# Moving where the pairs' hi and lo halves start in their tiles: 400 bytes below the whole tile's place instead of 64

## The chip, the cores and the metric

The kernel runs on one core of one Trainium2 chip. The metric is the device time of one launch in microseconds, over several runs. A profiled execution has its own time beside them, and a trace of every instruction of the engines: TensorE (PE, with its weight loads listed apart as PEld), VectorE (DVE), ScalarE (ACT), GpSimd (POOL) and SyncE (SP, which issues the DMAs).

## What is computed

One layer of an encoder on 256 tokens of width 4096, all in float32. The stream is layer-normed, multiplied by a wide input matrix, used in two branches (a gated convolution over three tokens, and windowed attention with 16 query heads), multiplied by an output matrix, added to the stream and normed again. Cut to what matters here:

```
h = layer_norm(x, emb_ln_g, emb_ln_b)              # 256 x 4096
p = h @ w_in                                       # 4096 x 13312 weights (26 column chunks of 512)
y_conv = c_b * conv3(c_c * c_h, conv_w) * silu(c_z)
y_attn = window_attention(q, k, v, sink) * silu(a_z)
y = concatenate([y_conv, y_attn]) @ w_out          # 4096 x 4096 weights
out = layer_norm(2**0.25 * h + y, ln_g, ln_b)
```

## The kernel before

Nearly all the work is the two products with `w_in` and `w_out`. The matrices arrive from memory in pieces of 128 x 2048 float32 (1 MB), each a tile `w0`, `w1`, ... of 8192 bytes in each of the 128 partitions. To keep float32 precision with the faster `float32r` matmul, every number is split in two: `hi`, the value rounded to float32r, and `lo`, what is left. ACT writes `hi` (`split_hi`, line 205) and DVE writes `lo = w - hi` (`split_lo`, line 209). The stream is split in the same way once and lies in `xT`. A product then takes three matmuls: x_hi by w_hi, x_hi by w_lo, x_lo by w_hi. In each, a 128 x 128 block of the stream is the stationary operand (the weights that PE loads), and 512 or 256 columns of `hi` or `lo` are the moving operand that streams past it.

Two kinds of steps follow each other in an order written out by hand (`ORDERS`, `OUT_ORDERS`):

- A whole step (`mm`, lines 251 to 253, and `mm_out`, lines 917 to 919) takes a whole piece of 2048 columns. In 512-wide column chunks that is 24 matmuls with 512 moving columns; in the last two output chunks, 256 columns wide, it is 48 matmuls with 256.
- A pair step (`mm_pair`, lines 275 to 277) multiplies two rows of blocks by a scheme with seven block products in place of eight. Its piece is loaded as four blocks of 256 columns, DVE adds four more blocks of sums beside them (`sums`, lines 182 to 184), and of the eight blocks the last seven (1792 columns) are split and used. The step is 21 matmuls with 256 moving columns. Their stationary operands are blocks of `xT` or of sums of it (`SC`, `SCy`).

Each chunk of the convolution branch is a row of whole steps (s), pair steps (S) and one half step (h): `sSShSsSSsSSs`. There are 185 pair steps in the kernel.

The `whi` and `wlo` tiles are three buffers each, used in turn, all of 8192 bytes. The split of step j + 3 stands behind the matmuls of step j on its engines, so ACT can write a `whi` buffer only when PE has finished with the step that used it, and DVE follows ACT.

The change touches where in these tiles a pair writes. Its seven blocks are read from column 256 (1024 bytes) of the `w` tile, and written `SHIFT` columns lower:

```
def dst(j, t):
    return t[:, HW - SHIFT:8 * HW - SHIFT] if is_pair(j) and len(raw[j].shape) == 2 else part(j, t)
...
c0 = HW if len(raw[j].shape) == 3 else HW - SHIFT
wh[j], wl[j] = wh[j][:, c0:c0 + 7 * HW], wl[j][:, c0:c0 + 7 * HW]
```

`HW` is 256, so with `SHIFT = 16` the seven blocks start at column 240 (960 bytes). A whole step's halves start at column 0. In the built program every `w`, `whi` and `wlo` buffer starts 384 bytes above a multiple of 512, and so does every stationary operand of these matmuls (the blocks of `xT`, `SC` and `SCy`).

Of the kernel before, what the change touches and what calls it, by code (L numbers as in the profile page):

```python
# [47 lines left out]
OP = 4  # L48
OUT_ORDERS = ["s" * 8] * 2 + ["sSsSsSsSss"] * 5 + ["", ""]
N_W = 3  # L50
SHIFT = 16


def units(ci):
# [45 lines left out]
def encoder_kernel(ctx: ExitStack, tc: tile.TileContext, x, emb_g, emb_b, wi, ws, conv_w, sink, wo, ln_g, ln_b, out):  # L100
# [85 lines left out]
    def part(j, t):  # L186

        if len(raw[j].shape) == 3:
            return t if len(t.shape) == 3 else t.rearrange("p (i n) -> p i n", i=2)
        return t[:, HW:] if is_pair(j) else t[:, 0:4 * HW] if steps[j][0] == "half" else t  # L190

    def dst(j, t):

        return t[:, HW - SHIFT:8 * HW - SHIFT] if is_pair(j) and len(raw[j].shape) == 2 else part(j, t)

# [11 lines left out]
    def split_lo(j):  # L207
        wl[j] = half_tile(j, "wlo")
        nc.vector.tensor_tensor(dst(j, wl[j]), part(j, raw[j]), dst(j, wh[j]).bitcast(F32), op=ALU.subtract)  # L209
        if is_pair(j):  # L210
            c0 = HW if len(raw[j].shape) == 3 else HW - SHIFT
            wh[j], wl[j] = wh[j][:, c0:c0 + 7 * HW], wl[j][:, c0:c0 + 7 * HW]
# [917 lines left out]
```

## Time and profile before

| | us |
|---|---|
| median of 3 runs | 1528.76 (1528.3 to 1529.1) |
| time of the profiled execution | 1529.49 |
| its span, first to last instruction | 1527.8 |
| PE busy, matmuls | 1511.7 (99%) |
| DVE busy | 1329.4 (87%) |
| ACT busy | 780.7 (51%) |

The clock granted to PE was 1.000 over the span. A matmul's busy time is longer than its place in the stream, because matmuls overlap and their ends are modelled: the distance from one matmul's start to the next one's start is what a matmul costs, and the timeline shows it.

### The profile page before, as it was taken

The page shows a single profiled execution, that of the slowest core. Times are in us where ns is not written, and L with a number is a line of the kernel's source. Part 1 is how long each engine was busy: PE and PEld are TensorE (multiplying, and loading weights), DVE is VectorE, ACT ScalarE, POOL GpSimd, SP SyncE. Part 2 cuts the span into 40 slices and gives each one's busy share as a digit, 9 for nine tenths or more (in the row PEclk, how much of TensorE's full clock was granted, in tenths as well). Part 3 has the DMA queues.
Part 4 walks back from the last instruction along what each step waited for, and adds up shares of the span by engine and source line. Part 5 has one row for each costly group of instructions (what it writes and reads, how often), then busy time and mean ns, then how long its engine had stood idle before and what let it go on. Part 6 is the DMA issues. An engine that isn't in the chain of part 4 may idle for free.

```text
span 1527.8 us, 21818 instructions
## 1 busy us (share of the span) xinstructions
PE 1511.7 (99%) x8879; PEld 1330.0 (87%) x8879; DVE 1329.4 (87%) x1555; ACT 780.7 (51%) x669; POOL 1.3 (0%) x7
## 2 busy tenths in 40 slices
PE   7999999999999999999999999999999999999998
PEld 4888989898988989989889888888988888888897
DVE  7769899999899898998898899989898688888876
ACT  5545546657565655545555455544556444444431
POOL 0000000000000000000000000000000000000000
PEclk9999999999999999999999999999999999999999
DMA  7555654555654556656555655556557655666573
GB/s 289 208 179 193 207 207 162 205 179 196 210 182 171 185 185 205 230 183 234 199 190 202 215 189 202 207 175 234 198 203 291 257 200 215 257 213 214 215 248 131
DMA packets 71716, 315.65 MB, mean 207 GB/s; under 512 B 8544, under 2 KB 12608, under 8 KB 50880
## 3 DMA queue, kind: packets, MB, share of 16 engines
q1 hardware_dynamic: 70608, 312.43, 58.4%
q10 hardware_dynamic: 1008, 1.84, 0.3%
q8 instruction: 69, 1.13, 0.3%
q14 instruction: 31, 0.25, 0.0%
HBM read 305.23 MB, written 8.91 MB: 206 GB/s over the span
## 4 chain that ended last, share of the span: by engine, by line
PE 83%; DVE 12%; ACT 2%; DMA 1%; issue 1%; SPq 0%; ACTq 0%; DVEq 0%
PE acc L252 13%; PE acc L253 13%; PE acc L251 13%; DVE wlo L209 7%; PE acc L918 6%; PE acc L919 6%; PE acc L917 6%; PE pacc L275 4%; PE pacc L277 4%; PE pacc L276 4%; PE acc L275 3%; PE acc L277 3%; PE acc L276 3%; ACT whi L205 2%; DVE w L182 1%
## 5 line engine op out<-in xcount | busy, mean ns | idle before, releaser
L205 ACT ACTIVATE whi<-w 128x2048 fp32r<-128x2048 f32 (+1 forms) x354 | 621.5, 1756 | 621.8 <-DVE w L184 218.2
L209 DVE TENSOR_TENSOR wlo<-w,whi 128x2048 fp32r<-128x2048 f32 (+1 forms) x354 | 736.4, 2083 | 123.7 <-ACT whi L205 123.5
L251 PE MATMUL acc<-whi,xT 128*128 128x512 f32 x988 | 387.4, 392 | 0.0
L252 PE MATMUL acc<-wlo,xT 128*128 128x512 f32 x988 | 386.0, 391 | 0.3
L253 PE MATMUL acc<-whi,xT 128*128 128x512 f32 x988 | 385.1, 390 | 0.0
L252 PEld LDWEIGHTS acc<-wlo,xT 128*128 128x128 f32 x988 | 185.5, 188 | 39.4 <-DVE wlo L209 3.6
L253 PEld LDWEIGHTS acc<-whi,xT 128*128 128x128 f32 x988 | 185.4, 188 | 38.1
L251 PEld LDWEIGHTS acc<-whi,xT 128*128 128x128 f32 x988 | 185.5, 188 | 35.0
L918 PE MATMUL acc<-wlo,xT 128*128 128x512 f32 (+1 forms) x480 | 175.1, 365 | 1.0 <-DVE wlo L209 1.0
L917 PE MATMUL acc<-whi,xT 128*128 128x512 f32 (+1 forms) x480 | 175.1, 365 | 0.0
L919 PE MATMUL acc<-whi,xT 128*128 128x512 f32 (+1 forms) x480 | 174.9, 364 | 0.0
L182 DVE TENSOR_TENSOR w<-w 128x512 f32<-128x512 f32 x179 | 122.3, 683 | 10.2 <-DMA w<-in_ws 10.2
L918 PEld LDWEIGHTS acc<-wlo,xT 128*128 128x128 f32 x480 | 90.6, 189 | 15.3 <-DVE wlo L209 1.7
L275 PE MATMUL acc<-whi,xT 128*128 128x256 f32 x370 | 103.7, 280 | 0.0
L276 PE MATMUL acc<-wlo,xT 128*128 128x256 f32 x370 | 103.7, 280 | 0.0
L277 PE MATMUL acc<-whi,xT 128*128 128x256 f32 x370 | 103.7, 280 | 0.0
L919 PEld LDWEIGHTS acc<-whi,xT 128*128 128x128 f32 x480 | 90.5, 189 | 14.3
L917 PEld LDWEIGHTS acc<-whi,xT 128*128 128x128 f32 x480 | 90.6, 189 | 13.9 <-issue 0.4
L275 PE MATMUL pacc<-whi,xT 128*128 128x256 f32 x350 | 99.8, 285 | 0.0
L276 PE MATMUL pacc<-wlo,xT 128*128 128x256 f32 x350 | 98.3, 281 | 0.0
L277 PE MATMUL pacc<-whi,xT 128*128 128x256 f32 x350 | 98.1, 280 | 0.0
L277 PE MATMUL pacc<-whi,SC 128*128 128x256 f32 x330 | 92.5, 280 | 0.0
(230 smaller groups left out, 2059.4 us busy)
## 6 DMA issues: line engine op xcount, KB each, us to landing
w<-in_wi SPq DMA_DIRECT2D x112, 1024.0 KB
w<-in_ws SPq DMA_DIRECT2D x202, 512.0 KB
w<-in_wo SPq DMA_DIRECT2D x41, 1024.0 KB
R<-in_wo SPq DMA_DIRECT2D x13, 1024.0 KB
x<-in_x SPq DMA_DIRECT2D x7, 512.0 KB
yl<-yd SPq DMA_DIRECT2D x7, 512.0 KB
xc<-in_x SPq DMA_DIRECT2D x14, 256.0 KB
R<-in_ws SPq DMA_DIRECT2D x6, 512.0 KB
```

The source lines that it names most:

```text
L182: nc.vector.tensor_tensor(s01, b22, b12.to_broadcast([P, 2, HW]), op=ALU.add)
L205: nc.scalar.activation(dst(j, wh[j]), part(j, raw[j]), AF.Copy)
L209: nc.vector.tensor_tensor(dst(j, wl[j]), part(j, raw[j]), dst(j, wh[j]).bitcast(F32), op=ALU.subtract)
L251: nc.tensor.matmul(a, xh, hk, start=(first and k == 0), stop=False)
L252: nc.tensor.matmul(a, xh, lk, start=False, stop=False)
L253: nc.tensor.matmul(a, xl, hk, start=False, stop=(last and k == PK - 1))
L275: nc.tensor.matmul(o, ah, hi[:, w - 1, :], start=(opens and p == 0), stop=False)
L276: nc.tensor.matmul(o, ah, lo[:, w - 1, :], start=False, stop=False)
L277: nc.tensor.matmul(o, al, hi[:, w - 1, :], start=False, stop=(closes and last))
L917: nc.tensor.matmul(o, yh, hk, start=first, stop=False)
L918: nc.tensor.matmul(o, yh, lk, start=False, stop=False)
L919: nc.tensor.matmul(o, yl, hk, start=False, stop=last)
```

## The change

One constant. A pair's `hi` and `lo` start at column 156 of their tiles (624 bytes) instead of column 240 (960 bytes). The same instructions stand in the same order on every engine, with the same waits; only the addresses differ that ACT and DVE write, that DVE reads of `whi`, and that PE reads as moving operand in the pairs' matmuls. Before, the moving operand of a pair's matmul starts 320 bytes above a multiple of 512 (64 bytes below the stationary operand's 384); now it starts 496 bytes above one (112 bytes above the stationary operand's). Before, it starts at a multiple of 64 bytes; now 48 bytes above one. Whole steps are as they were.

```
 OUT_ORDERS = ["s" * 8] * 2 + ["sSsSsSsSss"] * 5 + ["", ""]
 N_W = 3
-SHIFT = 16
+SHIFT = 100
```

## Prediction

> **What bounds the kernel.** I read the page first: busy times, then the chain of work that ended last, then the list of waits.
>
> ```profile
> PE 1511.7 (99%) x8879; PEld 1330.0 (87%) x8879; DVE 1329.4 (87%) x1555; ACT 780.7 (51%) x669; POOL 1.3 (0%) x7
> PE 83%; DVE 12%; ACT 2%; DMA 1%; issue 1%; SPq 0%; ACTq 0%; DVEq 0%
> ```
>
> ```profile
> ACT whi L205 <- PE acc L253: 172.7, 80, 3.7
> ...
> DVE wlo L209 <- ACT whi L205: 127.3, 101, 3.5
> ...
> PEld acc L252 <- DVE wlo L209: 3.6, 12, 0.4
> ```
>
> PE is busy 1511.7 of 1527.8 us. The waits turn in a ring: ACT waits for PE to give a `whi` buffer back (172.7 us here alone), DVE waits for ACT (127.3 us), and PE hardly waits for DVE (3.6 us in 12 waits). So the speed of the ring is PE's, and what a matmul costs in the stream is what counts. That is not its busy time but the distance between starts, so I went to the timeline of PE. First a pair step as most of them look, from its first matmul to the instruction behind it:
>
> ```profile
> 218.10 0.28 PE L275 MATMUL pacc<-whi,xT 128*128 128x256 f32 x1
> ...
> 218.45 0.28 PE L275 MATMUL acc<-whi,xT 128*128 128x256 f32 x1
> ...
> 220.45 0.28 PE L277 MATMUL pacc<-whi,SC 128*128 128x256 f32 x1
> 220.57 0.38 PE L490 MATMUL att<-ident,q 128*128 128x128 f32 x2
> ```
>
> Its 21 matmuls take 2.47 us. Between the fourth and the last start lie 17 steps in 2.00 us, 117.6 ns each. Now a pair step behind the attention's matmuls:
>
> ```profile
> 326.05 0.28 PE L275 MATMUL pacc<-whi,xT 128*128 128x256 f32 x1
> ...
> 326.40 0.28 PE L275 MATMUL acc<-whi,xT 128*128 128x256 f32 x1
> ...
> 328.33 0.28 PE L277 MATMUL pacc<-whi,SC 128*128 128x256 f32 x1
> 328.44 0.49 PE L490 MATMUL att<-ident,q 128*128 128x128 f32 x3
> ```
>
> The same code and the same addresses take 2.39 us, and the 17 steps take 1.93 us, 113.5 ns each. So a pair has two steady paces. Sorting all 185 pair steps by the median of their start distances gives 155 at the slow pace (117 to 118 ns) and 30 at the fast one (113 to 114 ns). The slow ones are those that PE enters straight out of a running stream of whole steps; the fast ones stand behind a break (a wait, transposes, the attention's matmuls). And here are matmuls of the same width, 256 columns, in a whole step of the last chunks, whose moving operand is not shifted:
>
> ```profile
> 1476.81 0.28 PE L917 MATMUL acc<-whi,xT 128*128 128x256 f32 x1
> ...
> 1478.49 0.28 PE L919 MATMUL acc<-whi,xT 128*128 128x256 f32 x1
> ```
>
> 14 steps in 1.68 us are 120.0 ns each, and they stay there. A whole step of 512 columns has one pace as well:
>
> ```profile
> 215.60 0.39 PE L252 MATMUL acc<-wlo,xT 128*128 128x512 f32 x1
> ...
> 217.87 0.39 PE L253 MATMUL acc<-whi,xT 128*128 128x512 f32 x1
> ```
>
> 10 steps in 2.27 us, 227 ns. From 120.0 to 227, 256 more columns cost 107 ns, so a 256-column matmul streams for some 107 ns and the rest is lost between or inside: 13 ns with the moving and the stationary operand at the same place modulo 512 bytes, 11 ns at the slow pace of the pairs, 6.5 ns at the fast one. My reading is that the next matmul's weight load, which runs under the current matmul's stream, gets in that stream's way where both reach for the same part of the memory, and that where they meet depends on the distance of their addresses and on the phase in which PE arrives.
>
> **The change part by part.** *PE, the moving operand's start.* 155 x 21 = 3255 matmuls at the slow pace and 630 at the fast one read from another place. No row shows a moving operand at this distance from the stationary one (112 bytes above, 48 past a multiple of 64), so the price is bounded. From below: no loss at all would be 107 ns. From the rows, the fastest steady pace is 113.5 ns. From above: 120.0 ns, the row at distance 0. I take the fast pace, 113.5 ns, because the current distance already admits it and only the phase in which the whole steps hand over keeps 155 pairs from it, and a distance that is no multiple of 64 puts the meeting points elsewhere; it is a choice between near rows, not a proof.
>
> The sum, by chunks of the convolution branch (7 pairs in 4 uninterrupted rows of one or two): the first pair of a row gains 2.47 - 2.39 = 0.08 us, since entering costs some slower matmuls; the three others gain 21 x (117.6 - 113.5) = 0.09 us. That is 0.59 us a chunk. The way back costs something. Here a whole step follows a fast pair:
>
> ```profile
> 223.30 0.28 PE L277 MATMUL pacc<-whi,SC 128*128 128x256 f32 x1
> 223.41 0.39 PE L251 MATMUL acc<-whi,xT 128*128 128x512 f32 x1
> ...
> 225.24 0.39 PE L253 MATMUL acc<-whi,xT 128*128 128x512 f32 x1
> ```
>
> Its first 8 steps take 1.83 us, where 8 x 0.227 = 1.82, so 0.01 to 0.03 us for each of 4 returns; 0.47 to 0.55 us a chunk are left. Behind 585 us, before the output, there are 89 slow pairs, 12.7 chunks' worth: 6.0 to 7.0 us. Before 585 us there are 46, or 6.6 chunks' worth: 3.1 to 3.6 us, of which I keep half, by the next paragraph: 1.6 to 1.8 us. In the output product 20 pairs stand one by one: 20 x (0.08 - 0.02) = 1.2 us. Together 8.8 to 10.0 us; I take 9.
>
> *What takes the place of PE's time.* A faster PE meets DVE next. The stretches of the attention, the convolution and the output:
>
> ```profile
> 252.00:378.00 126.00, 125.33 (x797) 113.10 (x796) 116.11 (x144) 80.00 (x86) 0.00 (x0) 1.00 0.58 196
> 924.00:1092.00 168.00, 167.93 (x1025) 150.09 (x1024) 151.97 (x166) 85.11 (x57) 0.00 (x0) 1.00 0.59 202
> 1260.00:1352.00 92.00, 92.00 (x495) 79.83 (x494) 80.94 (x87) 41.34 (x27) 0.00 (x0) 1.00 0.60 217
> ```
>
> The columns are the stretch, then busy us of PE, weight loads, DVE, ACT and POOL. In the convolution DVE has 16.0 us of 168 free, and PE would give back some 2 of them: it fits. In the attention DVE has 9.9 of 126 free, but its work comes in bursts and PE already loses 0.67 us there, so half is what I keep.
>
> *ACT and DVE, the new address.* 185 splits on each engine write from byte 624 instead of 960.
>
> ```profile
> L209 DVE TENSOR_TENSOR wlo<-w,whi 128x1792 fp32r<-128x1792 f32 x179 | 360.9, 2020 | 40.5 <-ACT whi L205 40.5
> L209 DVE TENSOR_TENSOR wlo<-w,whi 128x2048 fp32r<-128x2048 f32 x152 | 347.6, 2287 | 80.5 <-ACT whi L205 80.3
> ...
> L209 DVE TENSOR_TENSOR wlo<-w,whi 128x1024 fp32r<-128x1024 f32 x23 | 28.1, 1220 | 2.7 <-ACT whi L205 2.7
> ...
> L713 DVE SCALAR_TENSOR_TENSOR t<-att,cw,t 128x255 f32<-128x255 f32 x16 | 7.7, 483 | 0.6
> L711 DVE SCALAR_TENSOR_TENSOR t<-att,cw,t 128x255 f32<-128x255 f32 x16 | 7.6, 475 | 0.0
> ```
>
> A column costs (2287 - 1220) / 1024 = 1.042 ns; the shifted form should then take 1220 + 768 x 1.042 = 2020 ns, which it does. So the present shift between the `w` tile and the halves costs DVE nothing. Line 711 writes its tile from 4 bytes in, line 713 from its start, and the first is not slower (475 against 483 ns): an odd start costs DVE nothing either. I put both engines at 0, covered besides by the free time above; 1% on each split would be 20 ns of DVE in a pair and stay under that cover.
>
> **A rule weighed.** The rows above give one instruction stream 113.5, 117.6 or 120.0 ns at the same width. The Trainium skill ("SBUF — State Buffer", section "Who interferes with whom") gives PE two independent read ports, one for the moving operand and one for the weight load, and says that PE never waits on anyone; by that rule the address would not matter and the time would stay where it is. The trace speaks against it in so far as the pace differs between places, but no run yet moves the place alone. The Trainium skill ("TensorE: Matmul & The Clock Gate", section "Back-to-back issue gap") also gives 262 cycles for 256 columns, an estimate of 109 ns; by it the pairs could gain at most twice what I sum.
>
> **The rivals.**
>
> *The address is indifferent (1528.8 us).* Then 120.0 and 117.6 differ for another reason: the pairs write two halves of an accumulator in turn and change their moving block every matmul, the whole steps don't. For it: the slow pace of the pairs comes out the same for all their blocks and all their stationary operands. Against it: the two paces at one address show that something in the stream's phase costs 4 ns. It also holds if the interference repeats every 64 bytes or less and the rest of the shift is of no account. This is the rule of the two ports above.
>
> *The new place is as bad as none (slower, 1539 us).* If what matters repeats every 128 bytes, the old distance of 64 was the farthest from a meeting and the new one, 112, lies only 16 from one: the pairs then run at 120.0 ns like the unshifted row, with one pace only. Price: 3255 x (120.0 - 117.6) = 7.8 us and 630 x (120.0 - 113.5) = 4.1 us, together 11.9; of the second part some is hidden where PE waits for DVE anyway, so 10 us. It decides from 118.4 ns upwards (3885 x 0.8 ns = 3.1 us). A start that is no multiple of 64 bytes may also cost an additional access in each matmul. If one costs as much as the step from the fast to the unshifted pace, 6.5 ns, on top of the slow pace, that is 3885 x 6.5 = 25 us, 1554 us. I leave that end outside of the range.
>
> *More is gained.* With 107 ns the pairs would gain 3885 x 10 = 39 us by PE alone; DVE's free time would be used up long before (16.0 of 168 us), and a halved loss, 110 ns, would give some 17 us, 1512 us.
>
> **How the numbers follow.** Pairs at the fast pace or better: 0.44. Indifferent: 0.25. As bad as unshifted: 0.24; worse still: 0.07. A measurement of this kernel tells 0.2%, 3.1 us, from no change, so these are 0.44 faster, 0.25 same, 0.31 slower. The sum is made on the profiled execution (1529.49 us, 0.7 above the median of 1528.76): 9 us less than the median is 1519.8. For that case alone the range is 1512 to 1525; with the slower case it reaches from 1512 to 1540.
>
> **What would show it.** In the new trace the distance between starts in pair steps: 113.5 ns in those that follow whole steps means the forecast, 117.6 the first rival, 120.0 the second. The whole steps must stay at 227 ns and the splits at 2020 ns. If the pairs are at the fast pace and the time has not moved, waits of PE for `wlo` will have grown in its place. I am wrong if the interference has another period than I take it to have, which no row here can tell.

## The result, and the profile after

The changed kernel takes 1526.12 us (median of 22 runs, 1525.42 to 1526.76) where the kernel before takes 1528.78 (22 runs, 1528.01 to 1529.36). The ratio is 0.9983, with a 95% interval of 0.9976 to 0.9989: 2.66 us faster. That is 0.17%, a gain that can be told from none, but less than a third of the 9 us forecast. The profiled execution has a span of 1524.0 us, 3.8 below the one of before, at the same granted clock of 1.00.

The page, busy times and shares of the chain that ended last:

```profile
PE 1506.1 (99%) x8879; PEld 1320.3 (87%) x8879; DVE 1329.3 (87%) x1555; ACT 781.2 (51%) x669; POOL 1.3 (0%) x7
PE 81%; DVE 13%; ACT 2%; issue 1%; DMA 1%; SPq 0%; ACTq 0%; DVEq 0%
```

DVE's busy time has not changed, and its share of the chain went from 12 to 13%. First the pace, in the timeline of PE: the same pair step as the first one in the prediction, from its first matmul over the twelfth to the last.

```profile
217.76 0.28 PE L275 MATMUL pacc<-whi,xT 128*128 128x256 f32 x1
...
219.05 0.28 PE L277 MATMUL acc<-whi,xT 128*128 128x256 f32 x1
...
220.07 0.28 PE L277 MATMUL pacc<-whi,SC 128*128 128x256 f32 x1
...
223.06 0.39 PE L251 MATMUL acc<-whi,xT 128*128 128x512 f32 x1
...
224.90 0.39 PE L253 MATMUL acc<-whi,xT 128*128 128x512 f32 x1
```

It is entered straight out of whole steps. The first 11 distances average 1.29 / 11 = 117 ns, the last 9 are 1.02 / 9 = 113.3. So PE now finds the fast pace from there too, but not at once: about the first ten distances swing between 114 and 121 ns before they settle. Of 185 pairs 163 have a median of 113 to 114 ns (30 before), the other 22 lie at 115 to 118. The last two rows are the whole step behind the second pair of the row: 8 steps in 1.84 us, where 8 x 0.2267 is 1.81, so a return costs 0.03 us.

All of these 22 stand behind a break, and 18 of them were fast before. This is the pair behind the attention's matmuls that the prediction shows at 326.05, now with its first and twelfth matmul, its last, and the instruction behind it:

```profile
325.72 0.28 PE L275 MATMUL pacc<-whi,xT 128*128 128x256 f32 x1
...
327.02 0.28 PE L277 MATMUL acc<-whi,xT 128*128 128x256 f32 x1
...
328.04 0.28 PE L277 MATMUL pacc<-whi,SC 128*128 128x256 f32 x1
328.16 0.60 PE L490 MATMUL att<-ident,q 128*128 128x128 f32 x4
```

It took 2.39 us and takes 2.44: its first 11 distances average 1.30 / 11 = 118 ns, and only then does it reach 113.3. So the pairs that were fast already have become slower, by 0.04 us each in the mean of the 30.

The splits on DVE, groups with the shapes kept apart (busy us and mean ns behind the bar):

```profile
L209 DVE TENSOR_TENSOR wlo<-w,whi 128x1792 fp32r<-128x1792 f32 x179 | 360.9, 2020 | 38.7 <-ACT whi L205 38.7
L209 DVE TENSOR_TENSOR wlo<-w,whi 128x2048 fp32r<-128x2048 f32 x152 | 347.7, 2287 | 80.0 <-ACT whi L205 79.7
```

2020 and 2287 ns, as before. The new address costs DVE nothing. Now the waits (who waits, for whom; us in all, times, the longest in us), and behind them two rows of the kernel before that the prediction had no use for:

```profile
ACT whi L205 <- PE acc L253: 171.2, 80, 3.7
DVE wlo L209 <- ACT whi L205: 123.3, 94, 3.5
PEld acc L252 <- DVE wlo L209: 7.7, 27, 0.7
PE att L601 <- DVE s L567: 1.7, 4, 0.4
PEld att L616 <- DVE pT L608: 1.6, 5, 0.7
PE acc L252 <- DVE wlo L209: 1.5, 4, 0.4
```

```profile
PE att L601 <- DVE s L567: 1.3, 4, 0.3
PEld att L616 <- DVE pT L608: 1.2, 4, 0.6
```

PE's weight loads wait for `wlo` 27 times for 7.7 us, where it was 12 times and 3.6 us; its matmuls wait 4 times more, for 1.5 us. The attention's matmuls (lines 601 and 616) wait longer for DVE as well.

I summed the distances between the starts of all of PE's matmuls in both traces, by stretch: the pair steps without their waits, what a whole step has above 226.7 ns without a wait, the waits inside the products, and the other matmuls (attention, transposes) with their waits. The changes, in us:

| | attention | convolution | output | all |
|---|---|---|---|---|
| pair steps | -2.02 | -5.85 | -1.10 | -8.97 |
| waits inside the products | +0.49 | +3.12 | -0.68 | +2.94 |
| whole steps above their pace | +0.28 | +0.78 | +0.40 | +1.41 |
| other matmuls | +0.85 | +0.03 | -0.02 | +0.95 |
| together | -0.40 | -1.91 | -1.39 | -3.66 |
| forecast, returns taken off | -1.6 to -1.8 | -6.0 to -7.0 | -1.2 | -8.8 to -10.0 |

(The last column takes in 0.05 us of the prologue.) The row of the pair steps can't be held against the last row as it stands, since the forecast already has the returns taken off and half of the attention left out. Before that, the prediction's sum for the pair steps was 3.9 us in the attention (6.6 x 0.59), 7.5 in the convolution (12.7 x 0.59) and 1.6 in the output (20 x 0.08), 13.0 together; 8.97 came. Of these, 5.3 us were lost again, most of it as waits for DVE in the convolution.

One place shows how such a wait grows. Two timelines around one whole step of the convolution, the third step of a row of half step, pair and whole step. Before, DVE, ACT and PE:

```profile
960.50 0.42 DVE L184 TENSOR_TENSOR w<-w 128x256 f32<-128x256 f32 x1
...
962.84 2.02 DVE L209 TENSOR_TENSOR wlo<-w,whi 128x1792 fp32r<-128x1792 f32 x1 [0.77 <-ACT whi L205]
...
968.50 1.28 DVE L684 TENSOR_TENSOR tm<-acc,tm 128x512 f32<-128x512 f32 x2
```

```profile
961.10 1.71 ACT L205 ACTIVATE whi<-w 128x1792 fp32r<-128x1792 f32 x1 [1.75 <-DVE w L184]
```

```profile
968.18 0.39 PE L251 MATMUL acc<-whi,xT 128*128 128x512 f32 x1
968.64 0.50 PE L252 MATMUL acc<-wlo,xT 128*128 128x512 f32 x1
```

After, DVE and PE:

```profile
961.09 2.03 DVE L209 TENSOR_TENSOR wlo<-w,whi 128x1792 fp32r<-128x1792 f32 x1 [0.78 <-ACT whi L205]
...
964.55 2.29 DVE L209 TENSOR_TENSOR wlo<-w,whi 128x2048 fp32r<-128x2048 f32 x1
966.75 1.28 DVE L684 TENSOR_TENSOR tm<-acc,tm 128x512 f32<-128x512 f32 x2
```

```profile
966.12 0.40 PE L251 MATMUL acc<-whi,xT 128*128 128x512 f32 x1
966.89 0.50 PE L252 MATMUL acc<-wlo,xT 128*128 128x512 f32 x1 [0.37 <-DVE wlo L209]
```

From the point at which ACT lets it go, DVE works without a gap for 968.50 - 962.84 = 5.66 us before and 966.75 - 961.09 = 5.66 after: one pair's `lo`, the next pair's three sums, the whole step's `lo`. PE starts that whole step 5.34 us behind the same point before, and 5.03 after. It wants `wlo` one matmul later and gets it 5.80 us behind that point in both. The 0.31 us that PE gained on the way became 0.31 us of waiting. And the idle time ahead of DVE's stretch (0.77 and 0.78 us) is no reserve: the pair's sums end on DVE at 960.92, ACT makes `whi` of them from 961.10 to 962.81, and only then can DVE go on. It is ACT's passage in a chain from DVE to ACT and back to DVE.

### The profile page after: what moved, and what is told of

It is laid out like the page before. It is cut to its first block, busy times and chain, and to the rows that moved or that the text cites. A ratio compares the mean times of both kernels' runs of the same rounds, so it can differ in the third digit from the quotient of the medians.

```text
span 1524.0 us, 21818 instructions
## 1 busy us (share of the span) xinstructions
PE 1506.1 (99%) x8879; PEld 1320.3 (87%) x8879; DVE 1329.3 (87%) x1555; ACT 781.2 (51%) x669; POOL 1.3 (0%) x7
## 3 DMA queue, kind: packets, MB, share of 16 engines
q10 hardware_dynamic: 1008, 1.84, 0.3%
## 4 chain that ended last, share of the span: by engine, by line
PE 81%; DVE 13%; ACT 2%; issue 1%; DMA 1%; SPq 0%; ACTq 0%; DVEq 0%
PE acc L252 13%; PE acc L253 12%; PE acc L251 12%; DVE wlo L209 8%; PE acc L918 6%; PE acc L919 6%; PE acc L917 6%; PE pacc L277 4%; PE pacc L276 4%; PE pacc L275 4%; PE acc L276 3%; PE acc L275 3%; PE acc L277 3%; ACT whi L205 2%; DVE w L182 1%
## 5 line engine op out<-in xcount | busy, mean ns | idle before, releaser
L209 DVE TENSOR_TENSOR wlo<-w,whi 128x2048 fp32r<-128x2048 f32 (+1 forms) x354 | 736.4, 2083 | 120.6 <-ACT whi L205 119.6
```

## The experiments

Theory 1 was, at first, that the pairs gained what was forecast and that DVE's bursts took it back. Theory 2, that the loss lies elsewhere, so that the change would give as little on a kernel with less work for DVE.

**DVE relieved at the chunks' borders.** The adds that recombine the pairs, the convolution's side taps and the gate product are left out, and ACT copies the pairs' accumulators instead; once with the old place and once with the new.

```
     def pair_copy(ci):
-        nc.scalar.activation(e[:, 0, 0:HW], pacc[ci, 0][:, 0, :], AF.Copy)
+        for k in range(2):
+            nc.scalar.activation(e[:, k, :], pacc[ci, k].rearrange("p a b -> p (a b)"), AF.Copy)
     def pair_sums(ci):
-        ...
+        for k in range(2):
+            pacc.pop((ci, k))
```

> SHIFT 16 with DVE relieved: the recombination of the pairs' products (four adds of 256 columns a chunk), the two side taps of the convolution and the last gate product are left out; ACT copies the pairs' sums instead. Work on PE and the addresses stay. It is the base for the same kernel with SHIFT 100. Both theories: pairs as in the kernel before (155 at 117.8 ns, some 20 to 30 at 113.3), time 1520 to 1528 us, since PE waits little for DVE before the change.

> The same leaving out, SHIFT 100. Theory 1 (PE gave back 9 us in the pairs; where the convolution's chunks have their bursts of DVE work PE now waits 3.1 us longer for wlo, and 1.5 us go into the whole steps that follow a fast pair): with DVE relieved the waits do not grow, and it is 6 to 7.5 us faster than the relieved kernel with SHIFT 16. Theory 2 (the gain is lost in PE's own stream, by entering and leaving the fast pace, or in DMA): DVE's work is of no account, and the difference is 2.5 to 4 us as with the work in.

Measured: 1525.22 us (ratio 0.9977, interval 0.9967 to 0.9987) with the old place and 1521.77 (0.9954, 0.9942 to 0.9967) with the new, so the shift gives 3.45 us here, not the 6 to 7.5 of theory 1; that is a time of theory 2. DVE's busy time fell by 61 us, but PE's waits tell that it was not the time that counted. The row of each, old place first:

```profile
PEld acc L252 <- DVE wlo L209: 2.0, 7, 0.3
```

```profile
PEld acc L252 <- DVE wlo L209: 5.8, 30, 0.5
```

The waits inside the convolution's products grew with the shift again, from 2.50 to 4.52 us. What was left out stood at the chunks' borders, and the bursts in their middle stayed. With the waits still growing, this pair of runs does not decide between the theories, and the next pair was made to take DVE's work away where the waits are.

**DVE relieved inside the chunks.** As above, and `lo` is written for four of a pair's seven blocks only; the other three matmuls use those again.

```
+        if is_pair(j) and len(raw[j].shape) == 2:
+            nc.vector.tensor_tensor(dst(j, wl[j])[:, 0:4 * HW], part(j, raw[j])[:, 0:4 * HW],
+                                    dst(j, wh[j])[:, 0:4 * HW].bitcast(F32), op=ALU.subtract)
...
-            nc.tensor.matmul(o, ah, lo[:, w - 1, :], start=False, stop=False)
+            nc.tensor.matmul(o, ah, lo[:, (w - 1) % 4, :], start=False, stop=False)
```

> As the relieved kernel with SHIFT 16, and DVE's own work in the pairs cut too: lo is written for four of a pair's seven blocks only (1024 columns instead of 1792, about 0.8 us less per pair), and the matmuls of the other blocks read one of these four. PE's work and the places modulo 512 stay. Base for the next. Pairs as before (most at 117.8 ns); PE waits for wlo 1 us or less in the convolution; 1520 to 1526 us.

> The same leaving out, SHIFT 100. Theory 1 (the lost gain went into waits for the pairs' own splits, two pairs in a row giving DVE 7.1 us of work against 4.8 us of PE's): the waits stay below 1.5 us in the convolution and the difference to the lean kernel with SHIFT 16 is 6 to 7.5 us (9.0 in the pairs, less 1.5 for the returns). Theory 2 (the waits do not come from DVE's load): as with the work in, 2.5 to 4 us.

Measured: 1520.6 us (0.9943, 0.993 to 0.9957) and 1514.85 (0.9905, 0.9891 to 0.9918): the shift gives 5.75 us, twice what it gives in the full kernel and a little under the 6 to 7.5 expected. The chains of the two, old place first:

```profile
PE 98%; DVE 1%; DMA 0%; ACT 0%; SPq 0%; issue 0%; ACTq 0%
```

```profile
PE 99%; DMA 0%; DVE 0%; ACT 0%; issue 0%; SPq 0%
```

No wait of PE for `wlo` is left in the whole products of either. The waits in the products are the same with both places, to 0.04 us; the pair steps got 8.9 us shorter, the whole steps' returns from the fast pace cost 2.06 us more and the other matmuls 0.4. That leaves 6.5 us, close to the 6.6 by which the spans of the two profiled executions differ (1519.4 and 1512.8 us); the medians of all runs differ by 5.75. So with DVE's bursts out of the way the waits no longer take anything, and the change is worth 5.75 us; the forecast of 9 is not reached even then, because the pair steps give less than was summed for them.

**The unshifted place.** The prediction's second rival, run for itself.

```
-SHIFT = 16
+SHIFT = 0
```

> SHIFT 0: moving and stationary operand at the same place modulo 512 bytes in the pairs too. Theory 1 (the distance of the two operands sets the pace): all pairs at 120.0 ns with one pace, 9 to 11 us slower than before, 1538 to 1540 us. Theory 2 (the pairs' pace comes from their structure, and the place only tips the phase): 117.8 ns, time within 3 us of before.

Measured: 1534.49 us (1.0038, 1.0025 to 1.0051), 5.7 us slower than the kernel before. Timeline of PE, a pair's first matmul and the nineteenth, and then its shares of the chain and its wait for `wlo`:

```profile
219.03 0.28 PE L275 MATMUL pacc<-whi,xT 128*128 128x256 f32 x1
...
221.19 0.28 PE L275 MATMUL pacc<-whi,SC 128*128 128x256 f32 x1
```

```profile
PE 98%; DMA 1%; DVE 1%; ACT 0%; SPq 0%; issue 0%; ACTq 0%
```

```profile
PEld acc L252 <- DVE wlo L209: 0.2, 1, 0.2
```

18 steps in 2.16 us are 120.0 ns: the price that the prediction read off the 256-column whole steps. The pace is the one of theory 1, but the time lies between the two theories' ranges: the pairs got 9.8 us longer, and here too only a part arrives at the end, for the same reason turned round: a slower PE waits less (0.2 us for `wlo` where it was 3.6). DVE's share of the chain goes from 12 to 1%.

**Every distance, pairs.** To learn what sets the pace, each pair got its own place, 0, 4, 8 ... 252 columns below, one after the other.

```
-SHIFT = 16
+SHIFTS = [4 * k for k in range(64)]
...
+    shift = lambda j: SHIFTS[pair_no[j] % len(SHIFTS)]
```

> Each pair step has a SHIFT of its own, 0, 4, 8 ... 252 columns in turn, so that one trace gives the pace of 256 columns at 64 distances of moving and stationary operand. Theory 1 (the distance modulo some power of two sets the pace): the paces repeat in the distance, with 120 ns at 0, 117.8 or 113.3 at -64 bytes, 113.3 at -400, about 119 at 128 (= -384), and starts that are not multiples of 64 are not slower as such. Theory 2 (only the phase out of the step before counts): paces scatter without order in the distance.

1531.85 us, in a single run. The distance is the moving operand's start minus the stationary operand's, modulo 256 bytes; each appeared some 11 times, and distances 256 bytes apart agree. Every stationary operand of these steps starts at the same place modulo 512 bytes, here and in all other runs, so the distance stands as well for the moving operand's own start. Paces of pairs entered out of whole steps, as means of a pair's last 11 distances, in ns (at some places, 96 for one, single distances swing between 116 and 126):

| distance | 0 | 16 | 32 | 48 | 64 | 80 | 96 | 112 | 128 | 144 | 160 | 176 | 192 | 208 | 224 | 240 |
|---|---|---|---|---|---|---|---|---|---|---|---|---|---|---|---|---|
| ns | 120.0 | 118.5 | 116.6 | 118.4 | 117.7 | 119.6 | 119.9 | 113.3 | 119.7 | 116.5 | 118.5 | 119.4 | 117.7 | 118.9 | 118.5 | 117.3 |

A row of two pairs in its timeline; the first at distance 112, the second at 96. Shown are the tenth matmul of the first, then the first, the tenth and the last of the second:

```profile
902.17 0.28 PE L281 MATMUL acc<-whi,xT 128*128 128x256 f32 x1
...
903.53 0.28 PE L281 MATMUL pacc<-whi,xT 128*128 128x256 f32 x1
...
904.61 0.29 PE L281 MATMUL acc<-whi,xT 128*128 128x256 f32 x1
...
905.93 0.28 PE L283 MATMUL pacc<-whi,SC 128*128 128x256 f32 x1
```

12 steps in 1.36 us, 113.3 ns, and then, 16 bytes away, 11 steps in 1.32 us, 120.0 ns. 112 is the only one of the 16 that gives the fast pace to a pair entered out of whole steps. 192, the old place, gives it to a pair that follows another pair or a break (113.3 to 113.5) and 117.7 otherwise, and 144 gives it to a pair that follows another pair (113.3 to 113.4) and 116.5 out of whole steps: one address, two paces. Starts that are no multiple of 64 bytes cost nothing as such (distance 32 is faster than 64).

**The same distance by another shift.** 36 columns below is distance -144, which is 112 modulo 256 as well.

```
-SHIFT = 16
+SHIFT = 36
```

> Pairs written 144 bytes below instead of 400 (SHIFT 36). Both distances leave 112 modulo 256. Theory 1 (only the distance between the moving and the stationary operand modulo 256 bytes sets a pair's pace): pairs at 113.3 ns in every steady row, 1525 to 1527.5 us, within 1 us of the changed kernel. Theory 2 (the size of the shift matters, or the place modulo 512): pairs at another pace than 113 to 114 ns, 1528 to 1535 us.

Measured: 1526.62 us (0.9982, 0.9973 to 0.9991), 0.5 us from the changed kernel and with nearly the same ratio. The pair at the same point of its timeline, the twelfth and the last matmul:

```profile
219.28 0.28 PE L277 MATMUL acc<-whi,xT 128*128 128x256 f32 x1
...
220.30 0.28 PE L277 MATMUL pacc<-whi,SC 128*128 128x256 f32 x1
```

1.02 us again for 9 steps. Theory 1 holds: not the 400 bytes count but the place modulo 256. This trace is also a second sample of the accounting: waits inside the products of 2.93 us in the attention and 7.03 in the convolution (2.94 and 6.95 in the changed kernel), but 2.12 in the output, so the -0.68 in that column of the table is not of the change.

**The whole steps' distance.** The whole steps stand at distance 0, the worst place of a pair. Here every weight buffer moves 128 bytes up, and the pairs are not shifted.

```
-SHIFT = 16
+SHIFT = 0
...
+    const.tile([P, 32], F32, name="pad")
```

> SHIFT 0, but all weight buffers start 128 bytes later relative to xT, SC and SCy (an unused tile behind xT, the gap before SC smaller by as much), so whole steps and pairs both have their moving operand 128 bytes above the stationary one. Theory 1 (distance sets the pace, and a change of distance between steps costs the passage): no passages any more, pairs at 113.3 ns throughout, and whole steps below 227 ns, down to 213.3 + 6.7 = 220 ns; 4068 matmuls of 512 columns would give PE up to 27 us, of which DVE's free time (16 of 168 us) lets about half through: 1505 to 1518 us. Theory 2 (227 ns is what 512 columns cost at any place): whole steps stay at 227 ns; 1522 to 1528 us.

Measured: 1549.75 us (1.0137, 1.0123 to 1.0151), 21 us slower, where both theories expected a gain or none. A whole step in its timeline, the tenth matmul and the twenty-second:

```profile
218.09 0.39 PE L252 MATMUL acc<-whi,xT 128*128 128x512 f32 x1
...
220.89 0.39 PE L252 MATMUL acc<-whi,xT 128*128 128x512 f32 x1
```

12 steps in 2.80 us, 233 ns instead of 227. The place counts for 512 columns too, but the other way, so I mapped that as well: whole steps start 0, 16 ... 496 bytes up, pairs as in the changed kernel; the last 128 columns of a whole piece are left out, and its last block's matmuls read the block before.

```
+    up = lambda j: 4 * (whole_no[j] % 32) if len(raw[j].shape) == 2 and j < len(steps) - 1 else 0
...
+        return t[:, up(j):up(j) + cols(j)]
```

> SHIFT 100 in the pairs; each whole step's halves start 0, 16, 32 ... 496 bytes up in their tiles in turn (the last 128 columns are left out, and the last block's matmuls read the block before it), so that one trace gives the pace of 512 columns at 32 distances. Theory 1: the pace varies with the distance, from 220 ns (213.3 + 6.7, the loss of the fast pairs) to 235, with 227 at 0 and about 232 at 128, as measured with all buffers moved. Theory 2 (227 is the pace of 512 columns and 232 came from something else that moved): 227 at all distances.

1533.14 us, in a single run. Two whole steps, the first at distance 0 (its tenth matmul, and the first of the step behind it), the second at 240 (its fourth and twenty-second):

```profile
824.25 0.39 PE L266 MATMUL acc<-whi,xT 128*128 128x512 f32 x1
...
827.65 0.39 PE L266 MATMUL acc<-whi,xT 128*128 128x512 f32 x1
...
950.28 0.40 PE L266 MATMUL acc<-whi,xT 128*128 128x512 f32 x1
...
954.54 0.40 PE L266 MATMUL acc<-whi,xT 128*128 128x512 f32 x1
```

3.40 / 15 = 226.7 ns and 4.26 / 18 = 236.7. At 512 columns, distances 0 and 256 are the best of 32, the only ones at 226.7 in every whole step; 64 and 320 mostly take 229, most others 230 to 235, and 240 takes 226.7 in three steps and 236.7 in three others. A few more, such as 176 and 288, reach 226.7 in a single step. So the whole steps of this kernel already stand at their best place, and nothing is to be had there.

**Less work for DVE with nothing left out.** If DVE's time in the middle of a chunk is what lacks, the first of a pair's three sums can go to POOL, which has nothing to do.

```
-        nc.vector.tensor_tensor(s01, b22, b12.to_broadcast([P, 2, HW]), op=ALU.add)
+        nc.gpsimd.tensor_tensor(s01, b22, b12.to_broadcast([P, 2, HW]), op=ALU.add)
```

> The first of the three sums that a pair needs on its raw block (128x512) goes from DVE to POOL; nothing is left out; the halves lie 64 bytes below as before. It takes 179 x 684 ns = 122 us from DVE. Theory 1 (DVE's bursts hold back what a faster PE gives): as in the run that left DVE's sums out, 1524.5 to 1527 us. Theory 2 (DVE's share of time does not matter, or POOL and DVE hold each other up): 1528.5 us or more; DVE's split above 2040 ns would be the sign of the second.

> The same sum on POOL, with the halves 400 bytes below. Theory 1: DVE has the room now that it lacked, PE's waits for the lo half fall below 4 us in the convolution, and 1518 to 1522 us come out, 3.5 to 6 us below the same kernel with 64 bytes. Theory 2: no further below it than the change was by itself, 2.0 to 3.0 us, or both are slower than before because POOL is slow or in DVE's way.

Measured: 1542.23 us (1.0089, 1.0073 to 1.0106) and 1540.13 (1.0069, 1.0054 to 1.0084). Both are slower, and the shift gives 2.1 us here, as little as in the full kernel. Groups of the second:

```profile
L182 POOL TENSOR_TENSOR w<-w 128x512 f32<-128x512 f32 x179 | 322.8, 1806 | 912.2 <-DMA w<-in_ws 589.1 <-issue 66.6 <-DVE w L183 63.3
L183 DVE TENSOR_TENSOR w<-w 128x256 f32<-128x256 f32 x179 | 119.6, 668 | 20.6 <-POOL w L182 20.6
L209 DVE TENSOR_TENSOR wlo<-w,whi 128x1792 fp32r<-128x1792 f32 x179 | 389.2, 2175 | 47.1 <-ACT whi L205 47.1
```

POOL takes 1806 ns for what DVE did in 684, and DVE's own instructions get longer beside it: the second sum from 425 to 668 ns in the mean (half of them still take 418 or less, but 41 take more than 1000 and one 1542), the split from 2020 to 2175. Of the 122 us that DVE was to save, 44 and 28 are lost in these two rows alone, and it waits 20.6 us for POOL on top. This is the second sign that the expectation named. The Trainium skill ("SBUF — State Buffer", section "Who interferes with whom") says that a DVE instruction with two inputs in SBUF contends with a POOL instruction that reads SBUF; by that rule these two would slow each other, and these rows agree. So the pair of runs says nothing on whether DVE's bursts hold the gain back; it says that POOL isn't the way out.

**One instruction less at the border.** The two subtractions that recombine the pairs become one of 512 columns.

```
+            uv = e.rearrange("p i n -> p (i n)")[:, HW:3 * HW].rearrange("p (i n) -> p i n", i=2)
+            nc.vector.tensor_tensor(e[:, :, HW:W], p1[:, 1:2, :].to_broadcast([P, 2, HW]), uv, op=ALU.subtract)
```

> At the end of 28 chunks of the projections and the convolution the two subtractions that recombine the pairs become one of 512 columns; nothing is left out; the halves lie 400 bytes below. It takes one instruction of about 0.16 us from DVE in a chunk, 4 to 5 us of DVE in all, at the chunk's border. Theory 1 (what is missing is DVE's time in the middle of a chunk, and the border has slack): 1525 to 1526.5 us, no more than 1 us below the changed kernel. Theory 2 (any of DVE's time counts): 1521.5 to 1523.5 us.

The count in the expectation was too high: the five output chunks with pairs kept the old form, so 24 chunks have it. Measured: 1525.52 us (0.9975, 0.9964 to 0.9985), 1.1 us below the kernel with 36 columns that ran beside it, which takes the same paces. That is the border theory's time, at the upper end of what it allowed. The wait of PE for `wlo`:

```profile
PEld acc L252 <- DVE wlo L209: 6.7, 24, 0.5
```

6.7 us, where the two kernels with the old form have 7.6 and 7.7. It is the fastest of the kernels that compute everything, by little.

## Why the prediction was wrong

Two steps failed: the free time of DVE that was to take PE's gain, and, before it, the sum of what the pair steps give.

*The steady pace: right.* The pairs took the fast pace, 113.3 ns for the assumed 113.5. The reason given for it was right in part. The pace does hang on where the moving operand starts, which the first rival (an indifferent address) denied; the two maps rule that rival out, and with it the rule of the two independent ports in the Trainium skill ("SBUF — State Buffer", section "Who interferes with whom"), as far as the prediction drew from it that the address does not matter: at one width, 16 bytes apart, stand 113.3 and 119.9 ns. Whether it is the weight load that the stream meets, as the prediction reads it, is not shown: no run moved a stationary operand, so the distance of the two and the moving operand's own start were not told apart. And that 112 is fast because it "puts the meeting points elsewhere" was a guess, and lucky: of 16 distances modulo 256 it is the only one. The prediction could not tell the period (it weighed 64, 128 and 512 bytes), and the second rival, 120.0 ns at 112, was refuted by the run, but 96 bytes would have fulfilled it.

*The sum of the pair steps: mis-sized, 8.97 us for 13.0.* The second pairs of a row gained the 0.09 us that was summed (44 of them, 0.093 in the mean). But "the first pair of a row gains 2.47 - 2.39 = 0.08 us" took the price of entering from a pair that stood behind a break at the old place; out of whole steps at the new place, 106 pairs gained 0.055 in the mean, because about ten distances pass before the fast pace is reached. And the 630 matmuls of the 30 pairs that were already fast were put at nothing, though they move as well: these pairs lost 1.16 us in all. The bound "at most twice what I sum" is off too: worked out over all 3885 matmuls it comes to over three times the 9 us taken; the fastest pace in any run is 113.3 ns.

*The returns: right.* They were priced at 0.01 to 0.03 us each; the whole steps cost 1.41 us more in all, with 88 of them directly behind a pair.

*ACT and DVE at the new address: right.* 2020 and 2287 ns, unchanged.

*"In the convolution DVE has 16.0 us of 168 free, and PE would give back some 2 of them: it fits": this step failed.* The same stretch after the change:

```profile
924.00:1092.00 168.00, 167.53 (x1027) 148.89 (x1026) 152.40 (x168) 85.39 (x57) 0.00 (x0) 1.00 0.59 203
```

DVE is still free for 15.6 us of 168, and still PE's waits in the convolution's products rose from 3.83 to 6.95 us. A mean over 168 us says nothing about the 5.66 us in which DVE works without a gap, and part of the free time is ACT's passage inside the chain. A part could be seen beforehand, in a row that the prediction had: the wait of PE for `wlo`, 12 times, was small but not zero, and each stood at a place where DVE was already the later of the two. There whatever a pair gains is waited away. By the starts of PE's matmuls, about half of the growth in the convolution lies at such places, and the other half at some 16 places that had no wait before, where DVE must have been in time by less than what PE gained. Of the 6.0 to 7.0 us forecast for the convolution, 1.91 came: the pair steps less the returns gave 5.07, and 3.12 of that went into waits.

*Half kept in the attention: too much.* 1.6 to 1.8 us were kept and 0.40 came. The pair steps less the returns gave 1.74 there, which is the half that was kept, but by luck: they fell short because 24 of the 30 pairs that had been fast stand there (they lost 0.94 us) and most of the others are entered out of whole steps, and the waits that the half was meant to cover came on top, 0.49 in the products and 0.85 in the attention's own matmuls, which wait for DVE.

*The output: right in the number, by luck.* 1.2 us forecast, 1.39 measured. The pair steps less the returns gave 0.70; the rest is 0.68 of shorter waits, which the kernel with 36 columns does not have.

How far the cause is shown: the pair steps' shortfall is counted in the traces. For the waits, with DVE relieved at the places where they stand, the shift gives 5.75 us and no wait grows; relieved at the borders only, it gives 3.45 and the waits grow. The opposite change, a slower pace, loses 5.7 us of 9.8 because waits vanish. All three agree with DVE's bursts as the cause of the waits, and the first can hardly be read in another way. Not shown is a full kernel in which the bursts are gone; the one tried, with POOL, brought its own slowdown. Why 112 is fast stays open.

## What to carry to other kernels

When an engine at 99% gets faster, don't ask whether the second engine has free time in the mean; look at each place where the first already waits for it, however briefly, because there the whole local gain turns into waiting, and at those where the second is only just in time, and check whether the second engine's gaps are only the passage of another engine in its chain. A matmul stream that reloads its weights every time can have a pace that depends on where its moving operand starts; one profiled run with a different offset in each step maps it, for each width apart. Price a new place for every step that moves, the ones that are already fast too, and take the price of entering from rows that are entered in the same way. Expect a small gain of pace to cost something on the way back as well, where steps of another width follow.

## What the runs showed of the hardware

- The pace of 256-column matmuls with a weight load each lies between 113.3 and 120.0 ns when they are entered out of whole steps, by the moving operand's start modulo 256 bytes with the stationary operand's held at one place, and that of 512-column ones between 226.7 and 236.7. The best distance for the one (112) is not the best for the other (0).
- One address can have two steady paces: at distance 192 117.7 ns out of whole steps and 113.3 behind another pair or a break, and with 512 columns 226.7 and 236.7 at 240.
- An add of 128 x 512 float32 takes 1806 ns on POOL and 684 on DVE, and DVE's instructions with two inputs get slower beside it (425 to 668 ns and 2020 to 2175, in the mean).
